# Transposing the spatial gating's weights at the end of the first feed-forward sub-layer

## The chip, the cores and the metric

The kernel runs on one core of a Trainium2 chip. The metric is the device time of one execution in microseconds (us). TensorE multiplies and transposes, ScalarE and VectorE work on tiles, GpSimd does a few small things, and SP's queue issues all loads and stores. Each engine takes its own instructions strictly in order and waits for the others by semaphores.

## The reference

One decoder layer over 256 tokens of width 2048: a feed-forward sub-layer, a mixer, a second feed-forward sub-layer, each with a norm before and behind it. The change concerns one weight of the mixer, `w_spatial`, and the place between the first sub-layer and the mixer.

```python
def spatial_gating(u, v, ln_g, ln_b, w_sp, b_sp):
    v = layer_norm(v, ln_g, ln_b).reshape(b_, nc, L, N_GMLP_GROUPS, GMLP_GROUP)
    w_causal = w_sp * jnp.tril(jnp.ones((L, L), dtype=w_sp.dtype))
    z = jnp.einsum('gts,bnsgc->bntgc', w_causal, v) + b_sp.T[None, None, :, :, None]
    return u * z.reshape(b_, s_, D_GMLP)
...
        x = sublayer(x, 0, ffn(0), 0.5)
        x = sublayer(x, 1, mixer, 1.0)
        x = sublayer(x, 2, ffn(1), 0.5)
```

There are 8 groups of weights of 128 x 128. TensorE contracts over the partitions, so the kernel needs each group transposed, and masked so that a token sees only earlier ones.

## The kernel before

All large weights stream once from memory. A load of 512 KB or less lands in one of 8 raw buffers (`rawp`); ScalarE casts it to a high part `wh` (line 315), VectorE computes the remainder `wl` (line 320), and TensorE takes three products for each tile of 128 rows (lines 338 to 340, `mm3`). Two token tiles of 128 tokens (`t` = 0, 1) share each weight tile. Large tiles of the activations live in 9 slots (`Slot`, shown as `big`) that are handed out in the order in which they were freed. [...]

A scheduling layer turns the code into one list for each engine and sets the semaphores. It may change the order a little between neighbours, so the place of an instruction is read from the built order and not from the code alone.

`boundary` is the edge between two sub-layers. It runs the last products for token tile 0 (`last_mm(0)`), norms and updates the residual `xt` (`post_norm_t`, lines 452 and 464), and in the meantime loads the first weights of the next projection. Then come the last products for token tile 1 (`last_mm(1)`). Behind them the first half of the next input for tile 0 is transposed (`to_h`, line 423), scaled by VectorE (line 404) and ScalarE (line 402) and split into `hh` (cast, line 373) and `hl` (line 374). With this half the first products of the next projection begin, while tile 1 is being updated; its sum of squares (line 385) goes to GpSimd for the power that gives `rstd` (line 391), and the normed tile (line 415) goes the same way.

Behind the edge, and in the middle of the mixer's first products, stand the mixer's small preparations, among them the spatial weights: a load into a slot (line 776), eight transposes into two banks (line 780), two copies to `wst` (line 781) and the causal mask on GpSimd:

```python
    nc.gpsimd.affine_select(out=wst, in_=wst, pattern=[[0, 8], [1, P]], compare_op=ALU.is_ge,
                            fill=0.0, base=0, channel_multiplier=-1)
```

`wst` is first used in `spatial`, well behind this.

Of the kernel before, what the change touches and what calls it, by code (L numbers as in the profile page):

```python
# [8 lines left out]
F32 = mybir.dt.float32  # L9
# [5 lines left out]
P = 128  # L15
# [17 lines left out]
def tile_layer(  # L33
# [6 lines left out]
    nc = tc.nc  # L40
# [3 lines left out]
    w_in, w_out, conv_w, conv_b = w_in[0], w_out[0], conv_w[0], conv_b[0]  # L44
    b_igate, b_fgate, g_mhnorm = b_igate[0], b_fgate[0], g_mhnorm[0]
    gmlp_ln_g, gmlp_ln_b = gmlp_ln_g[0], gmlp_ln_b[0]
    w_spatial, b_spatial = w_spatial[0], b_spatial[0]
# [7 lines left out]
    rawp = ctx.enter_context(tc.tile_pool(name="rawp", bufs=8))  # L55
# [9 lines left out]
    def nm(s):  # L65
        uid[0] += 1
        return f"{s}_{uid[0]}"

    def ps():
        return psp.tile([P, 512], F32, tag="ps", name=nm("ps"))  # L70
# [29 lines left out]
    ident = cpool.tile([P, P], F32, name="ident")  # L100
# [194 lines left out]
    def flush():  # L295
        while pending:
            pump()
# [120 lines left out]
    def to_h(sub, t, q, n):  # L418

        for i in range(0, 4, 2):  # L420
            pn = ps()
            for j in range(2):
                nc.tensor.transpose(pn[:, j * P:(j + 1) * P], n[:, (i + j) * P:(i + j + 1) * P], ident)
            ins = modulate(sub, q * 4 + i, 2, pn, t * P, (t + 1) * P, i == 2)
        return ins
# [51 lines left out]
            tiles += [(2 * half + j, wh[:, j, :], wl[:, j, :]) for j in range(2)]  # L477
        return tiles

    def boundary(last_mm, evac, times_g, xin, y, yp, free, early, ahead, nxt, src=None, c0=None, w=512):  # L480

        kept = [] if nxt is None else early + list(w_tiles(src, [(4, 2 * ahead, 4)], c0, w=w))
        last_mm(0)
        evac(0)
        r = rstd_of(yp[0])
        r0 = post_norm_t(y, 0, r, times_g, nxt is None, xin)
        if nxt is None:
            last_mm(1)  # L490
            evac(1)
            r = rstd_of(yp[1])
            post_norm_t(y, 1, r, times_g, True, xin)
            return None
        if ahead == 1:
            floor[0] = last_update[0]
            kept += list(w_tiles(src, [(6, 2, 6)], c0, w=w))
        n0 = [normed(0, q, r0) for q in range(2)]
        last_mm(1)
        for s_ in free:  # L500
            s_.free()
        banks = [ps(), ps()]
        evac(1)
        r = rstd_of(yp[1])
        to_h(nxt, 0, 0, n0[0])
        to_h(nxt, 0, 1, n0[1])
        for k, wh, wl in kept:
            tok_mm(k, wh, wl, 0, banks[0][:, 0:w])
        r1 = post_norm_t(y, 1, r, times_g, False, xin)
        pq = [[ps(), ps()] for _ in range(2)]  # L510
        for q in range(2):
            n = normed(0, 2 + q, r0, last_update[0])
            for k in range(4):
                transposed_to(pq[q], k, 0, n)
        n1 = [normed(1, q, r1) for q in range(2)]
        to_h(nxt, 1, 0, n1[0])
        floor[:] = to_h(nxt, 1, 1, n1[1])
        for k, wh, wl in kept[:4]:
            tok_mm(k, wh, wl, 1, banks[1][:, 0:w])
        n = normed(1, 2, r1)  # L520
        for k in range(4):
            transposed_to(pq[0], k, 1, n)
        modulate_q(nxt, 2, pq[0], False)
        for k, wh, wl in kept[4:]:
            tok_mm(k, wh, wl, 1, banks[1][:, 0:w])
        n = normed(1, 3, r1)
        for k in range(4):
            transposed_to(pq[1], k, 1, n)
        modulate_q(nxt, 3, pq[1], False)
        for s_ in y + xin + gg:  # L530
            s_.free()
        gg[0] = None
        return banks, 2
# [43 lines left out]
        pending.append(rest())  # L577
        return g

    def ffn(idx, supers, begun, xin, nxt, nxt_src=None, nxt_c0=None, nxt_w=512):  # L580

        y = None
        yp = [parts() for _ in range(NT)]

        def evac_y(si, q, t, bank):
            ys = y[t].t[:, q * 512:(q + 1) * 512]
            if si == 0:
                nc.scalar.copy(ys, bank)
            else:
                nc.vector.tensor_tensor(out=ys, in0=ys, in1=bank, op=ALU.add)  # L590
            if si == len(supers) - 1:
                sumsq(yp[t], q, ys)

        for si, blocks in enumerate(supers):
            gs = []
            n = len(blocks)
            for b, segs, part, banks in blocks:
                if si == 0 and begun is not None and not gs:
                    gb = proj_tok(w_ff_gate[idx], b * FB, begun)
                    ub = proj_tok(w_ff_up[idx], b * FB)  # L600
                elif part is not None:
                    gb = proj_tok(w_ff_gate[idx], b * FB, segs=segs, first=segs[0][0])
                    ub = proj_tok(w_ff_up[idx], b * FB, segs=segs, first=segs[0][0])
                    flush()
                    gs.append(swiglu_sum(gb, ub, part))
                    continue
                else:
                    gb = proj_tok(w_ff_gate[idx], b * FB, segs=segs, banks=banks and banks[0])
                    ub = proj_tok(w_ff_up[idx], b * FB, segs=segs, banks=banks and banks[1])
                flush()  # L610
                gs.append(Slot((P, 2, 4, S), F32R))
                pending.append(swiglu_evac(gs[-1], gb, ub))
            if y is None:
                y = [Slot((P, D)) for _ in range(NT)] if xin[0].__class__ is Half else [Half(t) for t in range(NT)]
            rows = [(4 * i, 4, 4 * b[0]) for i, b in enumerate(blocks)]

            def mms(k, wh, wl, t):
                g = gs[k // 4].t
                mm3(banks[t], g[:, 0, k % 4, t * P:(t + 1) * P], g[:, 1, k % 4, t * P:(t + 1) * P],
                    wh, wl, k == 0, k == 4 * n - 1)  # L620

            for q in range(4):
                banks = [ps(), ps()]
                if si == len(supers) - 1 and q == 2:
                    for s_ in xin:
                        s_.t
                if si == len(supers) - 1 and q == 3:
                    flush()
                    if side[0] is not None:
                        side[0].drain()  # L630
                    early = early_w(nxt_src, nxt_c0, nxt_w)
                    kept, slots = hold(w_ff_down[idx], rows, q * 512, NW if nxt is None else 3)

                    def last_mm(t):
                        for k, wh, wl in kept:
                            mms(k, wh, wl, t)

                    return boundary(last_mm, lambda t: evac_y(si, q, t, banks[t]), lambda t: times_gg(y, t, q), xin, y, yp, slots + gs,
                                    early, 1, nxt, nxt_src, nxt_c0, nxt_w)
                else:  # L640
                    for k, wh, wl in w_tiles(w_ff_down[idx], rows, q * 512):
                        for t in range(NT):
                            mms(k, wh, wl, t)
                    for t in range(NT):
                        later(evac_y, si, q, t, banks[t])
                        if si == len(supers) - 1:
                            later(times_gg, y, t, q)
            if si < len(supers) - 1:
                for g in gs:
                    g.free()  # L650
# [67 lines left out]
    supers = [[], [], []]  # L718
# [34 lines left out]
    xin = [Reload(t) for t in range(NT)]  # L753

    blocks = [(4718, 410), (4308, 410), (3896, 412), (3484, 412), (G0, 412)]
    begun = ffn(0, supers, None, xin, 1, w_in, *blocks[0])
    side[0] = None


# [10 lines left out]
    lng = Slot((P, 2, DM))  # L770
    nc.sync.dma_start(lng.t[:, 0, :], gmlp_ln_g.partition_broadcast(P))
    nc.sync.dma_start(lng.t[:, 1, :], gmlp_ln_b.partition_broadcast(P))
    wst_s = Slot((P, 8, P))
    wst = wst_s.t
    wspr = Slot((P, 8, P))
    nc.sync.dma_start(wspr.t, w_spatial.rearrange("g t s -> t g s"))
    for i in range(2):
        pw = ps()
        for j in range(4):
            nc.tensor.transpose(pw[:, j * P:(j + 1) * P], wspr.t[:, i * 4 + j, :], ident)  # L780
        nc.scalar.copy(wst[:, i * 4:i * 4 + 4, :], pw.rearrange("p (g t) -> p g t", t=P))
    nc.gpsimd.affine_select(out=wst, in_=wst, pattern=[[0, 8], [1, P]], compare_op=ALU.is_ge,
                            fill=0.0, base=0, channel_multiplier=-1)
    wspr.free()
    gbias = cpool.tile([P, 8], F32, name="gbias")
    nc.sync.dma_start(gbias[:, 0:4], b_igate.partition_broadcast(P))
    nc.sync.dma_start(gbias[:, 4:8], b_fgate.partition_broadcast(P))
# [275 lines left out]
    yp = [parts() for _ in range(NT)]  # L1063
    y = None
# [20 lines left out]
    y = [Slot((P, D)) for _ in range(NT)]  # L1085
    for q in range(4):
# [8 lines left out]
        else:  # L1095
            flush()
            side[0].drain()
            early = early_w(w_ff_gate[1], 0, 512)
# [44 lines left out]
```

## Time and profile before

| | |
|---|---|
| median of 3 runs | 1872.24 us (1871.8 to 1872.76) |
| the profiled execution | 1872.83 us, of which the span of the instructions is 1870.8 |
| TensorE busy | 1823.0 us, 97% of the span |
| VectorE, ScalarE, GpSimd busy | 1365.0, 853.6, 22.5 us |
| loaded and stored | 499.82 MB, 267 GB/s in the mean |
| granted clock of TensorE | 0.999 of full speed in the mean |

Busy time is summed for each engine over the whole span. It does not say where an engine waited, or for whom; that is read stretch by stretch. Times in the rows below count from the start of the span.

### The profile page before, as it was taken

To read this page: it belongs to the slowest core of one execution; us is meant where nothing else is said; L and a number is where in the kernel's file an instruction comes from. 1 tells how busy PE (TensorE), PEld (TensorE's weight loads), DVE (VectorE), ACT (ScalarE), POOL (GpSimd) and SP (SyncE) were. 2 spreads that over 40 slices of the span, in tenths; PEclk is the share of its full clock that TensorE was granted. 3 is DMA by queue.
4 is the path that set the end of the run, shared out by engine and by line. 5 is a ranking of instruction groups with operands and counts; after the bars stand their busy time and mean duration, and the time that the engine had idled before them with its cause. 6 is when DMAs were issued, how large, how long until landed. Compare 5 with 4: busy or idle time off the path is not lost.

```text
span 1870.8 us, 23057 instructions
## 1 busy us (share of the span) xinstructions
PE 1823.0 (97%) x8501; PEld 1523.7 (81%) x8501; DVE 1365.0 (73%) x1479; ACT 853.6 (46%) x1058; POOL 22.5 (1%) x42
## 2 busy tenths in 40 slices
PE   3999999999999999999999999999999999999998
PEld 2888888888888888799988887888888888888886
DVE  6888798788987888868898987555556555556455
ACT  3555444444443444655545446444444444334443
POOL 1000000000000000000000000000000000000000
PEclk9999999999999999999999999999999999999999
DMA  9999889999899999578689994776677776677662
GB/s 346 346 359 342 314 293 318 319 307 322 294 331 323 340 306 334 188 240 278 218 288 306 358 342 141 221 223 213 228 228 221 221 223 214 219 228 220 190 190 91
DMA packets 232617, 499.82 MB, mean 267 GB/s; under 512 B 16828, under 2 KB 28332, under 8 KB 231992
## 3 DMA queue, kind: packets, MB, share of 16 engines
q1 hardware_dynamic: 232504, 498.36, 79.9%
q8 instruction: 66, 1.08, 0.2%
q14 instruction: 47, 0.39, 0.1%
HBM read 496.19 MB, written 2.10 MB: 266 GB/s over the span
## 4 chain that ended last, share of the span: by engine, by line
PE 86%; issue 8%; DVE 3%; DMA 2%; POOL 1%; ACT 0%; DVEq 0%; POOLq 0%; ACTq 0%; SPq 0%
PE ps L338 28%; PE ps L339 28%; PE ps L340 28%; DVE acc L172 2%; PE ps L542 1%; DVE wl L320 1%; DMA raw<-in_w_ada_dram 1%; DMA raw<-in_w_ff_up_dram 0%; POOL rstd L391 0%; DMA raw<-in_w_ff_gate_dram 0%; DMA xt<-in_x_dram 0%; PE ps L197 0%; PE ps L930 0%; ACT wh L315 0%; POOL brs L808 0%
## 5 line engine op out<-in xcount | busy, mean ns | idle before, releaser
L320 DVE TENSOR_TENSOR wl<-raw,wh 128x1024 fp32r<-128x1024 f32 (+2 forms) x635 | 766.1, 1210 | 450.3 <-ACT wh L315 449.3
L315 ACT CAST wh<-raw 128x1024 fp32r<-128x1024 f32 (+2 forms) x637 | 662.6, 1043 | 864.1 <-PE ps L340 737.0
L338 PE MATMUL ps<-wh,hh 128*128 128x512 f32 (+2 forms) x1680 | 650.3, 390 | 1.5 <-ACT hh L373 1.5
L339 PE MATMUL ps<-wl,hh 128*128 128x512 f32 (+2 forms) x1680 | 649.3, 387 | 1.2 <-DVE wl L320 1.2
L340 PE MATMUL ps<-wh,hl 128*128 128x512 f32 (+2 forms) x1680 | 649.1, 386 | 0.0
L339 PEld LDWEIGHTS ps<-wl,hh 128*128 128x128 f32 x1680 | 316.5, 188 | 61.9 <-DVE wl L320 2.7
L340 PEld LDWEIGHTS ps<-wh,hl 128*128 128x128 f32 x1680 | 316.1, 188 | 60.5
L338 PEld LDWEIGHTS ps<-wh,hh 128*128 128x128 f32 x1680 | 315.9, 188 | 60.1 <-ACT hh L373 1.7
L172 DVE SCALAR_TENSOR_TENSOR acc<-raw,cs,acc 128x1024 f32<-128x1024 f32 x270 | 345.1, 1278 | 0.8 <-DVE parts L389 0.4
L338 PE MATMUL ps<-wh,big 128*128 128x512 f32 x804 | 314.6, 392 | 0.0
L339 PE MATMUL ps<-wl,big 128*128 128x512 f32 x804 | 313.1, 389 | 0.2 <-DVE wl L320 0.2
L340 PE MATMUL ps<-wh,big 128*128 128x512 f32 x804 | 313.1, 389 | 0.0
L339 PEld LDWEIGHTS ps<-wl,big 128*128 128x128 f32 x804 | 151.0, 188 | 31.8 <-DVE wl L320 1.0
L340 PEld LDWEIGHTS ps<-wh,big 128*128 128x128 f32 x804 | 150.9, 188 | 31.7
L338 PEld LDWEIGHTS ps<-wh,big 128*128 128x128 f32 x804 | 150.9, 188 | 30.6
L338 PE MATMUL ps<-hh,wh 128*128 128x256 f32 x128 | 37.6, 293 | 0.0
L680 ACT COPY big<-ps 128x512 f32<-128x512 f32 x32 | 18.7, 589 | 40.8 <-PE ps L340 39.5
L374 DVE TENSOR_TENSOR big<-ps,big 128x512 fp32r<-128x512 f32 x52 | 35.5, 683 | 1.3 <-ACT big L373 1.2
L340 PE MATMUL ps<-hh,wl 128*128 128x256 f32 x128 | 36.2, 283 | 0.0
L339 PE MATMUL ps<-hl,wh 128*128 128x256 f32 x128 | 36.2, 283 | 0.0
L373 ACT CAST big<-ps 128x512 fp32r<-128x512 f32 x52 | 30.1, 578 | 0.0
L385 ACT ACTIVATE t<-xt 128x512 f32<-128x512 f32 x32 | 20.0, 626 | 17.7 <-DVE xt L590 9.6
(194 smaller groups left out, 751.4 us busy)
## 6 DMA issues: line engine op xcount, KB each, us to landing
raw<-in_w_ada_dram SPq DMA_DIRECT2D x224, 512.0 KB, 5.3
raw<-in_w_ff_gate_dram SPq DMA_DIRECT2D x176, 512.0 KB, 4.5
raw<-in_w_ff_up_dram SPq DMA_DIRECT2D x176, 512.0 KB, 4.5
raw<-in_w_ff_down_dram SPq DMA_DIRECT2D x176, 512.0 KB, 5.1
raw<-in_w_ada_dram SPq DMA_DIRECT2D x128, 256.0 KB, 5.5
raw<-in_w_in_dram SPq DMA_DIRECT2D x48, 512.0 KB, 5.1
raw<-in_w_out_dram SPq DMA_DIRECT2D x32, 512.0 KB
raw<-in_w_in_dram SPq DMA_DIRECT2D x24, 412.0 KB, 4.8
```

The lines of the kernel that those rows point to most:

```text
L172: ins = nc.vector.scalar_tensor_tensor(a, raw[:, j, :, :], cs[:, k:k + 1], a, op0=ALU.mult, op1=ALU.add)
L315: behind(nc.scalar.copy(wh, rawv), floor[1])
L320: last_split[0] = nc.vector.tensor_tensor(out=wl, in0=rawv, in1=wh.bitcast(F32), op=ALU.subtract)
L338: nc.tensor.matmul(o, lh, rh, start=start, stop=False, skip_group_check=True)
L339: nc.tensor.matmul(o, lh, rl, start=False, stop=False, skip_group_check=True)
L340: nc.tensor.matmul(o, ll, rh, start=False, stop=stop, skip_group_check=True)
L373: act = nc.scalar.copy(dh, src)
L374: return nc.vector.tensor_tensor(out=dl, in0=src, in1=dh.bitcast(F32), op=ALU.subtract), act
L385: nc.scalar.activation(junk, src, AF.Square, scale=float(D) ** -0.5, accum_out=p[:, q + q // 3:q + q // 3 + 1])
L542: nc.tensor.transpose(pg[:, j * S + t * P:j * S + (t + 1) * P], gts[t][:, m * P:(m + 1) * P], ident)
L680: nc.scalar.copy(part.t.rearrange("p k s -> p (k s)")[:, u * 1024 + i * 512:u * 1024 + (i + 1) * 512], banks[i])
```

## The change

The load of the spatial weights and the eight transposes are issued from within `boundary`, between `last_mm(1)` and the first `to_h`; the load goes to a raw buffer and no longer to a slot. The two copies to `wst` are issued behind the first two `to_h`. The mask stays where it was in the code. The lines that went are those of the old place.

```diff
--- before.py
+++ after.py
@@ -477,7 +477,7 @@
             tiles += [(2 * half + j, wh[:, j, :], wl[:, j, :]) for j in range(2)]
         return tiles
 
-    def boundary(last_mm, evac, times_g, xin, y, yp, free, early, ahead, nxt, src=None, c0=None, w=512):
+    def boundary(last_mm, evac, times_g, xin, y, yp, free, early, ahead, nxt, src=None, c0=None, w=512, between=None):
 
 
 
@@ -499,11 +499,14 @@
         last_mm(1)
         for s_ in free:
             s_.free()
+        rest = between() if between is not None else None
         banks = [ps(), ps()]
         evac(1)
         r = rstd_of(yp[1])
         to_h(nxt, 0, 0, n0[0])
         to_h(nxt, 0, 1, n0[1])
+        if rest is not None:
+            rest()
         for k, wh, wl in kept:
             tok_mm(k, wh, wl, 0, banks[0][:, 0:w])
         r1 = post_norm_t(y, 1, r, times_g, False, xin)
@@ -577,7 +580,7 @@
         pending.append(rest())
         return g
 
-    def ffn(idx, supers, begun, xin, nxt, nxt_src=None, nxt_c0=None, nxt_w=512):
+    def ffn(idx, supers, begun, xin, nxt, nxt_src=None, nxt_c0=None, nxt_w=512, between=None):
 
         y = None
         yp = [parts() for _ in range(NT)]
@@ -636,7 +639,7 @@
                             mms(k, wh, wl, t)
 
                     return boundary(last_mm, lambda t: evac_y(si, q, t, banks[t]), lambda t: times_gg(y, t, q), xin, y, yp, slots + gs,
-                                    early, 1, nxt, nxt_src, nxt_c0, nxt_w)
+                                    early, 1, nxt, nxt_src, nxt_c0, nxt_w, between)
                 else:
                     for k, wh, wl in w_tiles(w_ff_down[idx], rows, q * 512):
                         for t in range(NT):
@@ -753,7 +756,26 @@
     xin = [Reload(t) for t in range(NT)]
 
     blocks = [(4718, 410), (4308, 410), (3896, 412), (3484, 412), (G0, 412)]
-    begun = ffn(0, supers, None, xin, 1, w_in, *blocks[0])
+    wst_s = [None]
+
+    def spatial_weights():
+
+        wspr = rawp.tile([P, 8, P], F32, tag="raw", name=nm("wspr"))
+        nc.sync.dma_start(wspr, w_spatial.rearrange("g t s -> t g s"))
+        pws = [ps(), ps()]
+        for j in range(8):
+            nc.tensor.transpose(pws[j // 4][:, (j % 4) * P:(j % 4 + 1) * P], wspr[:, j, :], ident)
+
+        def rest():
+            wst_s[0] = Slot((P, 8, P))
+            for i in range(2):
+                nc.scalar.copy(wst_s[0].t[:, i * 4:i * 4 + 4, :], pws[i].rearrange("p (g t) -> p g t", t=P))
+
+        return rest
+
+    begun = ffn(0, supers, None, xin, 1, w_in, *blocks[0], between=spatial_weights)
+    wst_s = wst_s[0]
+    wst = wst_s.t
     side[0] = None
 
 
@@ -770,18 +792,8 @@
     lng = Slot((P, 2, DM))
     nc.sync.dma_start(lng.t[:, 0, :], gmlp_ln_g.partition_broadcast(P))
     nc.sync.dma_start(lng.t[:, 1, :], gmlp_ln_b.partition_broadcast(P))
-    wst_s = Slot((P, 8, P))
-    wst = wst_s.t
-    wspr = Slot((P, 8, P))
-    nc.sync.dma_start(wspr.t, w_spatial.rearrange("g t s -> t g s"))
-    for i in range(2):
-        pw = ps()
-        for j in range(4):
-            nc.tensor.transpose(pw[:, j * P:(j + 1) * P], wspr.t[:, i * 4 + j, :], ident)
-        nc.scalar.copy(wst[:, i * 4:i * 4 + 4, :], pw.rearrange("p (g t) -> p g t", t=P))
     nc.gpsimd.affine_select(out=wst, in_=wst, pattern=[[0, 8], [1, P]], compare_op=ALU.is_ge,
                             fill=0.0, base=0, channel_multiplier=-1)
-    wspr.free()
     gbias = cpool.tile([P, 8], F32, name="gbias")
     nc.sync.dma_start(gbias[:, 0:4], b_igate.partition_broadcast(P))
     nc.sync.dma_start(gbias[:, 4:8], b_fgate.partition_broadcast(P))
```

In the built order three places differ. Names are the program's: `ps` is a bank, `big` a slot, `t2` a scratch tile, `xt` the residual, and the numbers tell tiles apart.

ScalarE, behind the last update of token tile 0, before:

```order
L385 ACTIVATE t2_1312_6369,parts_351_1726<-xt_96 128x512
L402 ACTIVATE t2_1317_6386<-ps_1316_6383,bm_118,am_117 128x128
L373 CAST hh_115<-t2_1315_6378 128x2x128
L402 ACTIVATE t2_1317_6386<-ps_1316_6383,bm_118,am_117 128x128
L402 ACTIVATE t2_1321_6402<-ps_1320_6399,bm_118,am_117 128x128
L373 CAST hh_115<-t2_1317_6386 128x2x128
L373 CAST hh_115<-t2_1319_6394 128x2x128
L402 ACTIVATE t2_1321_6402<-ps_1320_6399,bm_118,am_117 128x128
L373 CAST hh_115<-t2_1321_6402 128x2x128
```

ScalarE at the same place, of the change:

```order
L772 COPY big_1325_6419<-ps_1311_6368 128x512
L385 ACTIVATE t2_1315_6381,parts_351_1726<-xt_96 128x512
L402 ACTIVATE t2_1320_6398<-ps_1319_6395,bm_118,am_117 128x128 x2
L373 CAST hh_115<-t2_1318_6390 128x2x128
L373 CAST hh_115<-t2_1320_6398 128x2x128
L373 CAST hh_115<-t2_1322_6406 128x2x128
L402 ACTIVATE t2_1324_6414<-ps_1323_6411,bm_118,am_117 128x128 x2
L772 COPY big_1325_6419<-ps_1312_6369 128x512
L373 CAST hh_115<-t2_1324_6414 128x2x128
```

One copy of the spatial weights now stands ahead of the sum of squares of token tile 1 (the row with `parts_351`), the other ahead of the last of the four casts to `hh`; and both `L402` of the first pair stand ahead of the first cast.

GpSimd, from the `rstd` of token tile 0 on, before (`big_1496` is `umask`, `big_1354` is `wst`, `big_1583` is `vv`):

```order
L391 TENSOR_TENSOR rstd_1304_6318<-parts_1299_6302,nhalf_94 128x1
L380 MEMSET parts_1323_6433 128x1
L843 AFFINE_SELECT big_1496_7330<-onesr_90 128x128
L391 TENSOR_TENSOR rstd_1313_6373<-parts_351_1726,nhalf_94 128x1
L380 MEMSET parts_1767_8834 128x1
L391 TENSOR_TENSOR rstd_1328_6449<-parts_1323_6433,nhalf_94 128x1
L380 MEMSET parts_1768_8836 128x1
L970 MEMSET big_1583_7977 128x8
L782 AFFINE_SELECT big_1354_6569<-big_1354_6569 128x1024
```

GpSimd at the same place, of the change (`wst` is `big_1325`):

```order
L855 AFFINE_SELECT big_1496_7330<-onesr_90 128x128
L391 TENSOR_TENSOR rstd_1304_6318<-parts_1299_6302,nhalf_94 128x1
L380 MEMSET parts_1327_6448 128x1
L391 TENSOR_TENSOR rstd_1316_6385<-parts_351_1726,nhalf_94 128x1
L380 MEMSET parts_1767_8834 128x1
L795 AFFINE_SELECT big_1325_6419<-big_1325_6419 128x1024
L982 MEMSET big_1583_7977 128x8
L391 TENSOR_TENSOR rstd_1332_6464<-parts_1327_6448,nhalf_94 128x1
L380 MEMSET parts_1768_8836 128x1
```

The mask of `umask` went ahead of the first of the three `rstd`, and the mask of `wst` and the fill of `vv` went ahead of the last of them.

SP's queue, at the old place of the load, before:

```order
L157 DMA raw_6722<-in_w_ada_dram 128x1024
L771 DMA big_6566<-in_gmlp_ln_g_dram 128x1024
L772 DMA big_6566<-in_gmlp_ln_b_dram 128x1024
L776 DMA big_6570<-in_w_spatial_dram 128x8x128
L304 DMA raw_6724<-in_w_in_dram 128x2x410
```

SP's queue at the new place, of the change:

```order
L304 DMA raw_6251<-in_w_in_dram 128x2x410
L304 DMA raw_6320<-in_w_in_dram 128x2x410
L764 DMA wspr_6366<-in_w_spatial_dram 128x8x128
L304 DMA raw_6591<-in_w_in_dram 128x2x410
L304 DMA raw_6609<-in_w_in_dram 128x2x410
```

The load of the spatial weights moved ahead of seven loads of `w_in`. On TensorE nothing else moved than the eight transposes, and on VectorE one `L464` went behind two `L374`.

## Rows read from the trace of the kernel before

**Rows 1.** The chain that ended last, shares of the span by engine (page, part 4).
```profile
PE 86%; issue 8%; DVE 3%; DMA 2%; POOL 1%; ACT 0%; DVEq 0%; POOLq 0%; ACTq 0%; SPq 0%
```

**Rows 2.** Stretches, TensorE to GpSimd: us, busy us (instructions); then granted clock, DMA share, GB/s.
```profile
780.00:782.40 2.40, 1.04 (x10) 0.80 (x8) 1.99 (x6) 1.42 (x5) 0.71 (x2) 1.00 1.06 300
782.40:787.14 4.74, 4.74 (x24) 4.33 (x24) 4.74 (x11) 4.04 (x12) 0.23 (x2) 1.00 0.78 256
787.14:791.20 4.06, 2.58 (x18) 1.69 (x17) 3.21 (x11) 1.90 (x7) 0.65 (x2) 1.00 0.00 0
791.20:801.80 10.60, 10.60 (x58) 9.91 (x58) 9.98 (x18) 9.84 (x19) 0.00 (x0) 1.00 0.36 89
```

**Rows 3.** Timeline of TensorE: start us, busy us, line, operation, tiles, [wait and releaser].
```profile
779.77 0.39 PE L340 MATMUL ps<-big,big 128*128 128x512 f32 x1
780.00 1.03 PE L423 MATMUL ps<-ident,t 128*128 128x128 f32 x8
782.40 0.45 PE L338 MATMUL ps<-hh 128*128 128x410 f32 x1 [1.36 <-ACT hh L373]
...
791.20 0.45 PE L338 MATMUL ps<-hh 128*128 128x410 f32 x1 [0.21 <-ACT hh L373]
...
802.09 1.09 PE L780 MATMUL ps<-ident,big 128*128 128x128 f32 x8
802.94 0.43 PE L340 MATMUL ps<-wh,hl 128*128 128x410 f32 x1
```

**Rows 4.** Timeline of ScalarE over the edge and at the copies.
```profile
780.98 0.63 ACT L385 ACTIVATE t<-xt 128x512 f32<-128x512 f32 x1 [3.15 <-DVE xt L590]
...
781.61 0.44 ACT L402 ACTIVATE t<-ps,bm,am 128x128 f32<-128x128 f32 x1
781.95 0.39 ACT L373 CAST hh<-t 128x256 fp32r<-128x256 f32 x1
...
802.78 1.07 ACT L781 COPY big<-ps 128x512 f32<-128x512 f32 x2 [0.27 <-PE ps L780]
```

**Rows 5.** Timeline of VectorE over the edge.
```profile
780.81 0.72 DVE L404 TENSOR_SCALAR t<-ps,am,bm 128x128 f32<-128x128 f32 x2
...
782.46 0.41 DVE L374 TENSOR_TENSOR hl<-t,hh 128x256 fp32r<-128x256 f32 x1
...
784.06 0.74 DVE L452 SCALAR_TENSOR_TENSOR xt<-xt,rstd,big 128x512 f32<-128x512 f32 x1
...
788.75 0.88 DVE L415 TENSOR_SCALAR t<-xt,rstd 128x512 f32<-128x512 f32 x2 [0.67 <-POOL rstd L391]
```

**Rows 6.** Timeline of GpSimd over the edge and at the mask.
```profile
778.41 0.55 POOL L391 TENSOR_TENSOR rstd<-parts,nhalf 128x1 f32<-128x1 f32 x1 [3.95 <-DVE parts L389]
...
780.25 0.29 POOL L843 TENSOR_SCALAR_AFFINE_SELECT big<-onesr 128x128 f32<-128x128 f32 x1 [1.12 <-PE ps L340]
...
788.16 0.55 POOL L391 TENSOR_TENSOR rstd<-parts,nhalf 128x1 f32<-128x1 f32 x1 [5.47 <-DVE parts L389]
...
803.93 1.27 POOL L782 TENSOR_SCALAR_AFFINE_SELECT big<-big 128x1024 f32<-128x1024 f32 x1 [0.57 <-ACT big L781]
```

**Rows 7.** Timelines of GpSimd and VectorE where two masks run.
```profile
895.75 1.18 POOL L891 TENSOR_SCALAR_AFFINE_SELECT t<-t 128x512 f32<-128x512 f32 x1 [43.31 <-DMA raw<-in_w_in_dram]
895.74 0.68 DVE L898 TENSOR_TENSOR t<-t,t 128x512 f32<-128x512 f32 x1
...
907.81 0.64 POOL L891 TENSOR_SCALAR_AFFINE_SELECT t<-t 128x512 f32<-128x512 f32 x1 [10.88 <-DMA raw<-in_w_in_dram]
907.94 1.05 DVE L898 TENSOR_TENSOR t<-t,t 128x512 f32<-128x512 f32 x1
```

**Rows 8.** SP's queue, and the DMA's busy tenths in 40 parts of 779 to 800.
```profile
760.68 9.83 SPq L304 DMA_DIRECT2D raw<-in_w_in_dram  x7
...
780.20 0.38 SPq L776 DMA_DIRECT2D big<-in_w_spatial_dram  x1
...
DMA  9699999899999500000000000000000095938694
```

## The prediction

> **What bounds the kernel now.** I read the chain that ended last first: 86% of it is TensorE and 2% a transfer [rows 1], so time is won or lost where TensorE stands still, or by what it is given to do. Then I cut the edge between the first feed-forward sub-layer and the mixer into stretches [rows 2], because everything the change touches lies there. The reader should see three things. From 780.00 to 782.40 TensorE works 1.04 us of 2.40. From 787.14 to 791.20 it works 2.58 of 4.06. From 791.20 to 801.80 it works 10.60 of 10.60, and VectorE (9.98) and ScalarE (9.84) are nearly full too. So there are two waits, and behind them a stretch paced by TensorE. The eight transposes of the spatial weights stand behind that, at 802.09 [rows 3].
>
> What ends each wait I took from the engines' timelines. The first ends at 782.40 with ScalarE's first cast to `hh` (781.95, 0.39 us) [rows 3, 4]. The second ends at 791.20, behind one long chain: VectorE runs without a hole to 787.14, 4.74 us of 4.74 (the casts' remainders `hl` from 782.46 on, the `L452` updates of the second token tile from 784.06), then the last sum of squares, GpSimd's `rstd` at 788.16, VectorE's `L415` at 788.75, transposes, modulation and cast [rows 2, 3, 5, 6].
>
> **The change, part by part.**
>
> *Removed at 802.* Eight transposes start at 802.09 and the next product at 802.94 [rows 3]. The stretch is TensorE's, so their going is worth 0.85 us. The bounds: nothing, if ScalarE or VectorE, both nearly full just before [rows 2], set the pace once TensorE has less to do; 1.09, their whole busy time. I take 0.85, since each loses work there too or keeps it: the two copies on ScalarE go (1.07 us) [rows 4].
>
> *Added at 780.* The last product starts at 779.77 and the first `to_h` transpose at 780.00 [rows 3]. The eight new ones go between, so `to_h` begins 0.85 later, at 780.85. Of this, most lies in the first wait, which is ScalarE's and VectorE's:
> - ScalarE. The first copy can start when four transposes are done, which took 0.69 before (802.09 to 802.78) [rows 3, 4]: at 780.69. A copy holds ScalarE 0.48 (two take 1.07, one 0.59). The sum of squares behind it moves from 780.98 to 781.18. After it the order now has both `L402` ahead of the first cast, not one, and one takes 0.34 (781.61 to 781.95) [rows 4]. The first cast goes from 781.95 to 781.18 + 0.63 + 2 x 0.34 = 782.49 and ends at 782.88. The first product follows 0.06 behind, at 782.94 for 782.40.
> - VectorE. Its first modulation needs two transposes. With 0.85 / 8 = 0.107 us for one, that is 0.69 - 2 x 0.107 = 0.48 after 780.85: 781.33, against 780.81 [rows 5]. The first remainder `hl` waits for the cast: 782.94 for 782.46, so 0.48 late. From there the same instructions follow without a hole, whatever their order, so the second wait ends 0.48 later.
>
> Bounds for this part: nothing, if the copies found holes; 0.85 + 0.48 = 1.33, if the transposes and a copy came in full. I take 0.48.
>
> *Moved on GpSimd.* This queue's order changes twice. The mask of `umask` (0.29 us, at 780.25) [rows 6] now stands ahead of the `rstd` that the transposes at 780.00 need. It waits for a product twelve places before the last; at 0.23 us each (779.77 to 780.00) [rows 3] that is about 777.5 with the product's own 0.39 us, so it ends near 777.8, and that `rstd` starts at 778.41 [rows 6]. Nothing is paid. The mask of the spatial weights `wst` (1.27 us, at 803.93) [rows 6] now stands ahead of the `rstd` that ends the second wait, with the small fill of `vv`, which waits only for an earlier `L464`. What is queued behind it is that `rstd`, and VectorE's `L415`, TensorE's transposes and all of the mixer wait for it. The mask starts when the second copy is done. That copy stands behind three casts and two more `L402`: 782.49 + 3 x 0.39 + 2 x 0.34 = 784.34 at the latest, done 0.59 later, so the mask begins by 785.0. The `rstd` is asked for at about 788.16 + 0.48. So in the queue alone there is room for 1.27 us.
>
> But a neighbour can be held up. A mask over 512 columns took 0.64 us at 907.81; VectorE's `L898`, begun 0.13 behind it, took 1.05 where the same instruction, begun first, took 0.68 at 895.74. There it was the mask that grew, to 1.18 [rows 7]. Each time the later one ended as if it had begun to read when the other ended: the two take turns at something. VectorE's `L452` reads two tiles as `L898` does and stands back to back with others of its kind from 784.06 on [rows 2, 5]. If the mask gets its turn between two of them, the chain grows by the time that it holds; if it gets none, it runs in the hole that VectorE leaves before `rstd`, and `rstd` comes that much later. Both land on the second wait. The price: 0.64 - 0.13 = 0.51 for 512 columns [rows 7], twice that, less a fixed part, for 1024: I take 0.95. Bounds: nothing (it fits into holes), and 1.27 (its row before).
>
> [...]
>
> *Moved on SP's queue.* The spatial weights' transfer, issued at 780.20, now stands where the first of seven `w_in` loads was, at 760.68, and takes one of eight raw buffers. Before, all transfers had landed 14 of 40 parts into the stretch 779 to 800, by 786.4, so this one took at most 6.2 us [rows 8]. From 760.68 that is 767, with 13 us to spare before 780.00. The loads behind it land a buffer later; the last now waits for a raw buffer to be split, as the `w_ada` load did, and is not among the tiles of this stretch. One `w_ada` load moves behind the new transposes; its sum is not needed in this stretch. Nothing is paid; without that cover each us of lateness would be a us of TensorE's.
>
> *Sum.* -0.85 + 0.48 + 0.95 = +0.58 us. The profiled execution took 1872.83 (span 1870.8 and 2.0 around it) and would take 1873.4. It stands 0.6 above the median of the three runs, 1872.24, so I predict 1872.8. Behind 803 every engine's order is the same as before, and TensorE paces the rest [rows 1], so the shift goes through to the end.
>
> **The rivals.**
> 1. The mask costs nothing, because it finds holes on VectorE. Then -0.85 + 0.48 = -0.37: 1871.9. For it: the holes that the 0.48 opens. Against it: there is none before 787.14 now [rows 2].
> 2. The transposes and copies too are hidden in the first wait (1.36 us stand empty there) and the change does what its place suggests: -0.85, 1871.4. Against it: the wait is ScalarE's, and the copies go onto ScalarE.
> 3. All comes in full: -0.85 + 1.33 + 1.27 = +1.75: 1874.0. For it: both engines are in one chain here.
> [...]
>
> **How the numbers follow.** A measurement of this kernel tells a change from none at about 0.2%, 3.7 us. I give the forecast 0.52, rival 1 0.25, rival 2 0.08, rival 3 0.10, rival 4 0.03, and 0.02 to a gain over 3.7 us, which would need more than half of both stretches (2.40 and 4.06 us) to go. So faster 0.02, same 0.95, slower 0.03. The forecast's own range is 1872.2 to 1873.5. The range over the cases takes in rivals 1 and 3, and with the spread of the three runs (0.96 us) reaches from 1871.2 to 1874.2.
>
> **What the profile after would show.** Right: eight transposes at about 780.0 without a wait before them, the first product near 782.9, the mask on GpSimd by 785.0 with either itself or one of VectorE's `L452`/`L374` beside it some 0.9 us longer than in the rows here, the first product behind the second wait near 792.6 for 791.20, and no transposes but one at 801.9. Wrong: a wait of TensorE ahead of the new transposes (the transfer), a clock below 1.00, a mask that grows by nothing beside unchanged `L452`, or new idle time on TensorE near 803, which would mean that the 0.85 was not TensorE's to give back.

## The result and the profile after

The changed kernel took 1887.92 us in the median of 6 runs (1887.25 to 1889.4), the kernel before 1872.26 beside it (1871.77 to 1872.86): a ratio of 1.0083 [1.0072, 1.0094], 15.7 us slower. Forecast was 1872.8, with a range that ended at 1874.2. The profiled execution of after took 1889.05, of which the span is 1887.0, 16.2 more than before's.

At the edge itself things went as forecast. The timeline of TensorE of after; columns as in [rows 3]:

```profile
783.76 0.39 PE L339 MATMUL ps<-big,big 128*128 128x512 f32 x1
...
786.03 0.39 PE L340 MATMUL ps<-big,big 128*128 128x512 f32 x1
786.26 1.03 PE L767 MATMUL ps<-ident,wspr 128*128 128x128 f32 x8
787.13 1.04 PE L423 MATMUL ps<-ident,t 128*128 128x128 f32 x8
789.14 0.45 PE L338 MATMUL ps<-hh 128*128 128x410 f32 x1 [0.98 <-ACT hh L373]
...
798.77 0.45 PE L338 MATMUL ps<-hh 128*128 128x410 f32 x1 [0.21 <-ACT hh L373]
...
809.21 0.35 PE L339 MATMUL ps<-wl,hh 128*128 128x410 f32 x1
809.49 0.26 PE L790 MATMUL ps<-ident,t 48*128 48x48 f32 x1
809.67 0.46 PE L340 MATMUL ps<-wh,hl 128*128 128x410 f32 x1
```

The new transposes follow the last product with no wait. But that product starts at 786.03, and in [rows 3] the same one starts at 779.77: **6.26 us were lost before the first instruction that the diff moves on TensorE**. From there the edge adds 809.67 - 802.94 - 6.26 = 0.47, where 0.58 was forecast. The rest is lost behind it, a little at a time: the shift is -0.1 at the start, 2.0 at 358, 6.3 at 780, 8.5 at 1101 and 15.7 at 1840 of before's time.

What is slower shows in the page's costliest groups (last columns: busy us, mean ns of one, idle before). Before:

```profile
L338 PE MATMUL ps<-wh,hh 128*128 128x512 f32 (+2 forms) x1680 | 650.3, 390 | 1.5 <-ACT hh L373 1.5
L338 PE MATMUL ps<-wh,big 128*128 128x512 f32 x804 | 314.6, 392 | 0.0
L339 PE MATMUL ps<-wl,big 128*128 128x512 f32 x804 | 313.1, 389 | 0.2 <-DVE wl L320 0.2
L340 PE MATMUL ps<-wh,big 128*128 128x512 f32 x804 | 313.1, 389 | 0.0
```

And after:

```profile
L338 PE MATMUL ps<-wh,hh 128*128 128x512 f32 (+2 forms) x1680 | 650.1, 390 | 1.5 <-ACT hh L373 1.5
L338 PE MATMUL ps<-wh,big 128*128 128x512 f32 x804 | 319.4, 398 | 0.0
L339 PE MATMUL ps<-wl,big 128*128 128x512 f32 x804 | 318.1, 396 | 0.0
L340 PE MATMUL ps<-wh,big 128*128 128x512 f32 x804 | 317.9, 395 | 0.0
```

Products whose weights (the stationary operand) lie in `hh` are the same. The 2412 whose weights lie in a slot grew by 4.8 + 5.0 + 4.8 = 14.6 us, with no idle time before them. Measured from one start to the next, as they are paced, they went from 227 to 233 ns in the mean, 2412 x 6.2 ns = 15.0 us. Nothing in the diff names these products; they are those of `w_ff_down` and of the output projection, all over the program.

**What differs for them is an address.** One large tile, `vv`, is 8224 bytes long in each partition, the other slot tiles are at most 8192, and slot number 4 has a pool of its own for it:

```python
    VSLOT = 4
...
            self.i = free_slots.pop(0)
            pool = bigv if self.i == VSLOT else big
```

The changed kernel takes one slot fewer (the raw spatial weights), so by its turn `vv` gets slot 0, which lies first in `big` and grows from 8192 to 8224 bytes. By the addresses of the two built programs, the slots behind it then start 32 bytes higher (the first of them at 90272, not 90240), and so do the raw buffers, the scratch tiles and the pool of slot 4; `hh`, `hl` (from 16512 on), `wh` and `wl` (from 49280) stay. Slot 0 itself keeps its place, but in the changed kernel no product has its weights there.

### The profile page after: what moved, and what is told of

It is laid out like the page before. It is cut to its first block, busy times and chain, and to the rows that moved or that the text cites. A ratio compares the mean times of both kernels' runs of the same rounds, so it can differ in the third digit from the quotient of the medians.

```text
span 1887.0 us, 23058 instructions
## 1 busy us (share of the span) xinstructions
PE 1839.3 (97%) x8501; PEld 1525.3 (81%) x8501; DVE 1365.7 (72%) x1479; ACT 852.1 (45%) x1058; POOL 22.8 (1%) x42
## 4 chain that ended last, share of the span: by engine, by line
PE 88%; issue 8%; DVE 2%; DMA 1%; ACT 1%; POOL 1%; DVEq 0%; POOLq 0%; ACTq 0%
PE ps L338 28%; PE ps L340 28%; PE ps L339 28%; DVE acc L172 1%; PE ps L545 1%; DMA raw<-in_w_ada_dram 1%; DVE wl L320 0%; DMA xt<-in_x_dram 0%; ACT t L402 0%; POOL rstd L391 0%; DMA raw<-in_w_in_dram 0%; PE ps L440 0%; PE ps L197 0%; PE ps L942 0%; POOL brs L820 0%
## 5 line engine op out<-in xcount | busy, mean ns | idle before, releaser
L338 PE MATMUL ps<-wh,hh 128*128 128x512 f32 (+2 forms) x1680 | 650.1, 390 | 1.5 <-ACT hh L373 1.5
L339 PE MATMUL ps<-wl,hh 128*128 128x512 f32 (+2 forms) x1680 | 649.3, 386 | 1.2 <-DVE wl L320 1.2
L340 PE MATMUL ps<-wh,hl 128*128 128x512 f32 (+2 forms) x1680 | 649.5, 387 | 0.0
L339 PEld LDWEIGHTS ps<-wl,hh 128*128 128x128 f32 x1680 | 316.5, 188 | 62.3 <-DVE wl L320 2.7
L340 PEld LDWEIGHTS ps<-wh,hl 128*128 128x128 f32 x1680 | 315.9, 188 | 60.5
L338 PEld LDWEIGHTS ps<-wh,hh 128*128 128x128 f32 x1680 | 316.0, 188 | 59.8 <-ACT hh L373 1.7
L338 PE MATMUL ps<-wh,big 128*128 128x512 f32 x804 | 319.4, 398 | 0.0
L339 PE MATMUL ps<-wl,big 128*128 128x512 f32 x804 | 318.1, 396 | 0.0
L340 PE MATMUL ps<-wh,big 128*128 128x512 f32 x804 | 317.9, 395 | 0.0
L340 PEld LDWEIGHTS ps<-wh,big 128*128 128x128 f32 x804 | 151.0, 188 | 36.4
L339 PEld LDWEIGHTS ps<-wl,big 128*128 128x128 f32 x804 | 151.1, 188 | 36.3 <-DVE wl L320 0.8
L338 PEld LDWEIGHTS ps<-wh,big 128*128 128x128 f32 x804 | 151.0, 188 | 35.4
L338 PE MATMUL ps<-hh,wh 128*128 128x256 f32 x128 | 37.6, 293 | 0.0
L374 DVE TENSOR_TENSOR big<-ps,big 128x512 fp32r<-128x512 f32 x52 | 35.5, 684 | 1.3 <-ACT big L373 1.2
L340 PE MATMUL ps<-hh,wl 128*128 128x256 f32 x128 | 36.2, 283 | 0.0
L339 PE MATMUL ps<-hl,wh 128*128 128x256 f32 x128 | 36.2, 283 | 0.0
L391 POOL TENSOR_TENSOR rstd<-parts,nhalf 128x1 f32<-128x1 f32 x12 | 7.6, 631 | 1620.4 <-DVE parts L389 1620.4
```

The costliest lines, as they stand in the source:

```text
L338: nc.tensor.matmul(o, lh, rh, start=start, stop=False, skip_group_check=True)
L339: nc.tensor.matmul(o, lh, rl, start=False, stop=False, skip_group_check=True)
L340: nc.tensor.matmul(o, ll, rh, start=False, stop=stop, skip_group_check=True)
L374: return nc.vector.tensor_tensor(out=dl, in0=src, in1=dh.bitcast(F32), op=ALU.subtract), act
L391: nc.gpsimd.tensor_tensor(out=r, in0=p[:, 6:7], in1=nhalf[:, 0:1], op=ALU.pow)
```

## Experiments

Each time stands beside runs of the kernel before on the same chip. In the kernels with paddings line numbers are one to four higher (L338 is L339, L340 or L342). Where there are two paddings of 32 bytes, what lies behind the second is 64 bytes higher, so it keeps its place against a multiple of 64.

**1. The change with the old layout.** `vv` keeps a pool of its own, whichever slot it gets.

```diff
-    VSLOT = 4
+    VSLOT = 0
```

> The change as it is, but with the oversized slot (8224 bytes a partition, for `vv`) put where `vv` now lands, so that every slot and raw buffer stands at the address that it had before. Theory A (32 bytes of address): products with weights from a slot go back from 233 to 227 ns apart, the time to 1872.26 + 0.48 = 1872.7 (1872.2 to 1873.5), and the edge still costs what the prediction's walk gave. Theory B (the move itself, its transfer, its waits or a fall of the clock that it causes): 1888 as the change. Theory C (only the edge, without the mask on GpSimd in the way): 1871.9.

1873.72 us, ratio 1.0005 [0.9997, 1.0014]: no change that can be measured. The median is 0.2 above the range that was expected, and far from the 1888 of theory B. The 15 us are the layout's. This trace (span 1870.7) gives the forecast's terms without the drift; TensorE's timeline:

```profile
779.10 0.39 PE L340 MATMUL ps<-big,big 128*128 128x512 f32 x1
779.33 1.03 PE L767 MATMUL ps<-ident,wspr 128*128 128x128 f32 x8
780.20 1.04 PE L423 MATMUL ps<-ident,t 128*128 128x128 f32 x8
782.21 0.46 PE L338 MATMUL ps<-hh 128*128 128x410 f32 x1 [0.98 <-ACT hh L373]
...
791.84 0.45 PE L338 MATMUL ps<-hh 128*128 128x410 f32 x1 [0.20 <-ACT hh L373]
...
802.75 0.45 PE L340 MATMUL ps<-wh,hl 128*128 128x410 f32 x1
```

Against [rows 3], counted from the last product (779.10 for 779.77, so 0.67 is added to each): `to_h` 0.87 late, the first product 0.48, the end of the second wait 1.31, the first product behind the old place 0.48.

**2. The mask behind all three `rstd`** (with the old layout).

```diff
-    nc.vector.tensor_copy(v3, pt[:, 0:48])
+    v3_copy = nc.vector.tensor_copy(v3, pt[:, 0:48])
...
-    nc.gpsimd.affine_select(out=wst, in_=wst, pattern=[[0, 8], [1, P]], compare_op=ALU.is_ge,
-                            fill=0.0, base=0, channel_multiplier=-1)
+    behind(nc.gpsimd.affine_select(out=wst, in_=wst, pattern=[[0, 8], [1, P]], compare_op=ALU.is_ge,
+                                   fill=0.0, base=0, channel_multiplier=-1), v3_copy)
```

> As e1_vslot, and the mask of `wst` on GpSimd behind the three `rstd` of the edge. If the mask holds up VectorE in the edge as the prediction's third term says, 0.9 us less than e1_vslot: 1871.8. If that term is empty, the same as e1_vslot.

1872.2 us, ratio 1.0000 [0.9992, 1.0009]. In the trace the same four landmarks are 0.88, 0.49, 0.81 and 0.08 late. The mask now meets VectorE's `L415`; GpSimd and VectorE:

```profile
789.61 1.36 POOL L795 TENSOR_SCALAR_AFFINE_SELECT big<-big 128x1024 f32<-128x1024 f32 x1
789.53 1.72 DVE L415 TENSOR_SCALAR t<-xt,rstd 128x512 f32<-128x512 f32 x2 [0.67 <-POOL rstd L391]
```

Two `L415` take 1.72 for the 0.88 of [rows 5], but TensorE's second wait ends only 0.81 - 0.49 = 0.32 later, for 0.83 in experiment 1. So the mask's place is worth 0.5 us at the second wait (1.31 - 0.81) and 0.4 at the last landmark (0.48 - 0.08), and it is not free at this one.

**3. Transposes behind `to_h`, copies behind the first products** (and the mask late, the old layout).

```diff
-        rest = between() if between is not None else None
...
         to_h(nxt, 0, 1, n0[1])
-        if rest is not None:
-            rest()
+        rest = between() if between is not None else None
         for k, wh, wl in kept:
             tok_mm(k, wh, wl, 0, banks[0][:, 0:w])
+        if rest is not None:
+            rest()
```

> As e8_mask_late, and the eight transposes behind the two `to_h`, in TensorE's empty 1.36 us, with the copies behind the first casts. If the second term (0.48) is what transposes and copies ahead of `to_h` cost, the whole 0.85 of the removal is left: 1871.4. If the 0.85 is not TensorE's to give back, 1872.3.

1872.16 us, ratio 0.9998 [0.9989, 1.0007]. TensorE's timeline:

```profile
779.39 1.04 PE L423 MATMUL ps<-ident,t 128*128 128x128 f32 x8
780.26 1.04 PE L767 MATMUL ps<-ident,wspr 128*128 128x128 f32 x8
781.78 0.45 PE L338 MATMUL ps<-hh 128*128 128x410 f32 x1 [0.49 <-ACT hh L373]
```

The landmarks are 0.0, 0.0, 0.5 late and at last 0.24 early: the eight transposes fit into the first wait. The second wait is still late, and two `L415` take 1.71 beside the mask here too, so the whole 0.85 that was expected of this form does not come. This is the best form of the change that the runs give, and its gain is far below what a measurement of this kernel can tell.

**4. The kernel before with the change's layout.** Paddings of 32 bytes ahead of `big` and ahead of the constants; slots, raw buffers and scratch tiles all lie 32 higher.

```diff
+    pad0 = ctx.enter_context(tc.tile_pool(name="pad0", bufs=1))
+    pad0.tile([P, 8], F32, name="gap0")
     big = ctx.enter_context(tc.tile_pool(name="big", bufs=1))
...
+    pad1 = ctx.enter_context(tc.tile_pool(name="pad1", bufs=1))
+    pad1.tile([P, 8], F32, name="gap1")
     cpool = ctx.enter_context(tc.tile_pool(name="cpool", bufs=1))
```

> The kernel before, nothing moved, with 32 unused bytes a partition ahead of the slots: slots, raw buffers, scratch tiles and sums stand 32 bytes higher, as in the change. Theory A: 2412 products with weights from slots at 6.2 ns more each, 15.0 us, so 1887.3 (1886.5 to 1888). Theory B: 1872.3, as before.

1888.34 us, ratio 1.0084 [1.007, 1.0098]: the whole loss, without a line of the change (0.3 above the range expected).

**5. The slots alone.** The second padding stands ahead of the raw buffers.

```diff
+    pad0.tile([P, 8], F32, name="gap0")
     big = ...
+    pad1.tile([P, 8], F32, name="gap1")
     rawp = ...
```

> The kernel before with the eight slots alone 32 bytes higher, all behind them back on multiples of 64. If it is the slots (weights of TensorE's products): +15 us, 1887. If it is the raw buffers or scratch tiles (casts, remainders, transfers): 1872.3.

1887.53 us, ratio 1.0079 [1.0064, 1.0094].

```profile
L342 PE MATMUL ps<-wh,big 128*128 128x512 f32 x804 | 319.5, 398 | 0.0
```

**6. All but the slots**: raw buffers, scratch and `w_ada` tiles 32 higher.

```diff
+    pad0.tile([P, 8], F32, name="gap0")
     rawp = ...
+    pad1.tile([P, 8], F32, name="gap1")
     bigv = ...
```

> The kernel before with raw buffers, scratch tiles and sums alone 32 bytes higher, the slots where they were. If it is the slots: 1872.3. If it is the raw buffers or scratch tiles: 1887.

1873.89 us, ratio 1.0006 [0.9996, 1.0015]. So it is the slots, and not the raw buffers or scratch tiles that ScalarE, VectorE and the transfers read and write.

```profile
L342 PE MATMUL ps<-wh,big 128*128 128x512 f32 x804 | 314.8, 392 | 0.0
```

**7. `hh` and `hl` alone** 32 off.

```diff
+    pad0.tile([P, 8], F32, name="gap0")
     hpool = ...
+    pad1.tile([P, 8], F32, name="gap1")
     wsp = ...
```

> The kernel before with `hh` and `hl` alone 32 bytes off a multiple of 64. They are the weights (the operand that is loaded) of about 5090 products of 410 to 512 columns. If any weights 32 bytes off cost 6.2 ns a product: +31 us, 1904. If it is something of the slots alone: 1872.3.

1899.84 us, ratio 1.0145 [1.0128, 1.0162]. `wh`, `wl` and the slots lie 64 higher here, so `hh` lies 32 lower against the streaming operand and the slots lie at no distance. Now it is the other products, one line of three each:

```profile
L342 PE MATMUL ps<-wh,hh 128*128 128x512 f32 (+2 forms) x1680 | 658.3, 394 | 1.5 <-ACT hh L377 1.5
L342 PE MATMUL ps<-wh,big 128*128 128x512 f32 x804 | 314.7, 392 | 0.0
```

The loss is 27.0 where some 31 were expected. The 456 products of 410 and 412 columns were counted in, and they did not slow down: the median from one start to the next is 187 ns for those of 410, before and here. One form of them, before and in this experiment:

```profile
L338 PE MATMUL ps<-wh,hh 128*128 128x412 f32 x96 | 33.5, 349 | 0.0
```

```profile
L342 PE MATMUL ps<-wh,hh 128*128 128x412 f32 x96 | 33.5, 349 | 0.0
```

**8. `wh` and `wl` alone**, the streaming operand of both kinds of product.

```diff
+    pad0.tile([P, 8], F32, name="gap0")
     wsp = ...
+    pad1.tile([P, 8], F32, name="gap1")
     big = ...
```

> The kernel before with `wh` and `wl` alone 32 bytes off. They are the operand that streams through in nearly all products of 512 columns, and the weights in 384 of 256 columns. If the weights' address matters and the streaming operand's doesn't: +0 to +2.4 us (384 x 6.2 ns), 1872.3 to 1874.7. If the streaming operand's address matters as much: some 7400 products x 6.2 ns, +46 us, 1918.

1915.0 us, ratio 1.0223 [1.0208, 1.0238]: both kinds are slow, and the loss, 42.2, is close to that of experiments 5 and 7 together (14.7 + 27.0 = 41.7). The slots lie 64 higher here, so they are 32 higher than the streaming operand, and `hh` is 32 lower.

```profile
L342 PE MATMUL ps<-wh,hh 128*128 128x512 f32 (+2 forms) x1680 | 658.4, 395 | 1.5 <-ACT hh L377 1.5
L342 PE MATMUL ps<-wh,big 128*128 128x512 f32 x804 | 319.4, 398 | 0.0
```

My first theory, that weights at such an address are slow, fell here: the weights lie where they were against a multiple of 64, and the products are slow. Two were left: any operand that lies off is slow, or the two operands must lie alike (theory C).

**9. All operands of the products 32 higher.**

```diff
+    pad0.tile([P, 8], F32, name="gap0")
     hpool = ...
+    pad1.tile([P, 8], F32, name="gap1")
     cpool = ...
```

> The kernel before with every tile of the products, streaming operand (wh, wl) and both kinds of weights (hh, hl and slots) alike, 32 bytes higher. Theory C (a product of 512 columns takes 233 ns for 227 when its streaming operand and its weights lie differently modulo 64 bytes): nothing differs any more, products 227 ns, 1872.3, within 1.5. Rival (any operand that is 32 off in itself makes the product slow): all products 233 ns, 1915 or more, as with wh and wl alone.

1873.03 us, ratio 0.9999 [0.999, 1.0008]. Every operand is off, and nothing is slow:

```profile
L342 PE MATMUL ps<-wh,hh 128*128 128x512 f32 (+2 forms) x1680 | 649.8, 389 | 1.5 <-ACT hh L377 1.5
L342 PE MATMUL ps<-wh,big 128*128 128x512 f32 x804 | 314.5, 392 | 0.0
```

**10. `wh`, `wl` and the slots 32 higher.**

```diff
+    pad0.tile([P, 8], F32, name="gap0")
     wsp = ...
+    pad1.tile([P, 8], F32, name="gap1")
     rawp = ...
```

> The kernel before with wh, wl and the slots 32 bytes higher, hh and hl where they were. Theory C (streaming operand and weights differ): only the products with hh and hl as weights differ and take 233 ns, those with slots 227; the time is that of hh and hl alone being moved, 1899.8, within 2. Rival (any operand off): both kinds at 233 ns, 1915 as with wh and wl alone.

1898.94 us, ratio 1.0138 [1.0121, 1.0154]. The same slots that are slow in experiment 5 are fast once `wh` and `wl` are moved along with them:

```profile
L342 PE MATMUL ps<-wh,hh 128*128 128x512 f32 (+2 forms) x1680 | 658.6, 395 | 1.5 <-ACT hh L377 1.5
L342 PE MATMUL ps<-wh,big 128*128 128x512 f32 x804 | 314.6, 392 | 0.0
```

It is the distance of the two operands that counts. The next four ask modulo what.

**11. The slots 64 higher** (paddings as in 5, of 16 elements in place of 8).

```diff
-    pad0.tile([P, 8], F32, name="gap0")
+    pad0.tile([P, 16], F32, name="gap0")
```

> The kernel before with the slots alone 64 bytes higher. If the place modulo 64 decides: products with slots 227 ns, 1872.3, within 1.5. If the place modulo 128 (or any difference) decides: 233 ns, 1887.5, as with 32 bytes.

1887.76 us, ratio 1.0078 [1.0063, 1.0093]: my guess of 64 in theory C fell.

**12. The slots 128 higher**, with all behind them.

```diff
+    pad0.tile([P, 32], F32, name="gap0")
     big = ...
```

> The kernel before with the slots (and everything behind them) 128 bytes higher, wh, wl, hh and hl where they were. If the difference between streaming operand and weights counts modulo 128 bytes: products with slots 227 ns, 1872.5, within 1.5. If it counts modulo more, or if any difference counts: 233 ns, 1887.5, as with 32 and 64 bytes.

1885.61 us, ratio 1.0067 [1.005, 1.0084]. Still slow, if a little less. All large products of the kernel before lie at a distance of 0 modulo 512, which led to theory D.

**13. The slots 256 higher.**

```diff
-    v2 = cpool.tile([P, 64], F32, name="v2")
+    v2 = pad0.tile([P, 64], F32, name="v2")
```

> The kernel before with the slots 256 bytes higher (the 256 bytes are one small tile, v2, that lay behind them). Theory D (products are fast where weights and streaming operand start at the same place modulo 512 bytes, as all large products of the kernel before do): 256 apart is slow, 232 to 233 ns, 1885 to 1888. Rival (modulo 256): 227 ns, 1872.5, within 1.5.

1872.23 us, ratio 0.9998 [0.9989, 1.0008]. Theory D's 512 fell; 256 will do. The lines of experiments 11, 12 and 13:

```profile
L342 PE MATMUL ps<-wh,big 128*128 128x512 f32 x804 | 319.2, 398 | 0.0
```

```profile
L340 PE MATMUL ps<-wh,big 128*128 128x512 f32 x804 | 318.9, 397 | 0.0
```

```profile
L339 PE MATMUL ps<-wh,big 128*128 128x512 f32 x804 | 314.6, 392 | 0.0
```

**14. The slots 512 higher.**

```diff
-    ident = cpool.tile([P, P], F32, name="ident")
+    ident = pad0.tile([P, P], F32, name="ident")
```

> The kernel before with the slots 512 bytes higher (the 512 bytes are the identity, which lay behind them). Theory D (modulo 512): 227 ns, 1872.5, within 1.5. Rival (the slots must not be moved at all, or the distance counts modulo more than 512): 232 to 233 ns, 1885 to 1888.

1873.23 us, ratio 1.0003 [0.9993, 1.0012]. The line of experiment 13 reads the same here.

All of it in one table; the distance is that of weights from streaming operand, modulo 256, and ns are the mean from one start to the next for products of 512 columns, intervals of 300 ns and more left out:

| kernel | distance: `hh`, slots | ns: `hh`, slots | us more than before |
|---|---|---|---|
| before, 1 to 3, 6, 9, 13, 14 | 0, 0 | 227, 227 | -0.6 to 1.1 |
| after, 4, 5 | 0, 32 | 227, 233 | 14.7 to 15.7 |
| 11 | 0, 64 | 227, 233 | 14.7 |
| 12 | 0, 128 | 227, 232.6 | 12.6 |
| 7, 10 | -32, 0 | 233, 227 | 27.0, 25.9 |
| 8 | -32, 32 | 233, 233 | 42.2 |

## Why the prediction was wrong

**The step that failed** is at its start and its end: that "everything the change touches lies there", at the edge, and that "Behind 803 every engine's order is the same as before, and TensorE paces the rest [rows 1], so the shift goes through to the end". The order is indeed the same, and TensorE does pace it. But an order says which instruction comes next, not where its operands lie, and I took their durations for given: the sum has no term for them, and no reason is given why it should be nothing. The runs showed 14.6 us in its place, 2412 products at about 6 ns more each. The change took a slot out of the rotation, `vv` moved into another, and that changed the size of a slot and the address of all behind it. Experiment 1 takes this away and the loss is gone; experiment 4 puts it alone into the kernel before, and the loss is there. None of the rivals was about memory.

**The terms at the edge held**, by the trace of experiment 1, with after's (less 6.26) the same within 0.02:
- Removed at 802: 0.85 forecast, 1.31 - 0.48 = 0.83 measured (0.73 and 0.74 in experiments 2 and 3).
- Added at 780: the transposes delay `to_h` by 0.87 (0.85 forecast), the first product by 0.48 (0.48 was taken; 782.94 - 782.40 = 0.54 on its own row). ScalarE's first copy began in after at 786.89, which is 780.63, forecast 780.69.
- The mask: 0.95 forecast, 1.31 - 0.48 = 0.83 measured. It was `L374` that was held; GpSimd and VectorE of after:

```profile
790.96 1.48 POOL L795 TENSOR_SCALAR_AFFINE_SELECT big<-big 128x1024 f32<-128x1024 f32 x1 [1.83 <-ACT big L772]
791.40 1.31 DVE L374 TENSOR_TENSOR hl<-t,hh 128x256 fp32r<-128x256 f32 x1
```

One `L374` takes 0.41 in [rows 5], here 1.31, so 0.90 more (0.42 in experiment 2, with the mask behind it); and the mask began at 790.96 - 6.26 = 784.70, "by 785.0". Rival 1 (nothing) and rival 3 (all 1.27) are both off. That 0.95 came so near was partly luck: in [rows 7] `L898` grew by 1.05 - 0.68 = 0.37, and not by the 0.51 that the prediction took from there, and where in the mask its victim would begin, on which the price hangs, was not worked out. What was left of the mask was 0.51 in [rows 7] and is 1.48 - 0.44 = 1.04 here; both times the other instruction grew by 0.14 less than that. `L374` began 0.44 into the mask's 1.48 and ended 0.27 behind it. The `L452` ahead of it, which ran beside the mask's first 0.5, from 790.74 on, took 0.75, for 0.74 in [rows 5]. So the price is below the mask's whole time.
- The sum: +0.58 forecast, +0.48 in experiment 1. Its median lies 1.0 above before's, with an interval of the ratio (0.9997 to 1.0014) that holds both 0 and the sum.
- The transfer was in time: no wait ahead of `L767`.
- Rival 4, the one with 0.03, stood for a fall of TensorE's clock at this edge. Neither before's nor after's trace shows one there. The stretches of after that answer to [rows 2]:

```profile
786.26:789.14 2.88, 1.91 (x17) 1.67 (x15) 2.14 (x7) 2.25 (x7) 0.65 (x2) 1.00 0.94 289
789.14:793.98 4.84, 4.83 (x24) 4.33 (x24) 4.84 (x9) 3.35 (x10) 1.53 (x2) 1.00 0.54 202
793.98:798.77 4.79, 2.45 (x17) 1.66 (x17) 3.94 (x13) 2.63 (x10) 0.65 (x2) 1.00 0.00 0
798.77:808.50 9.73, 9.73 (x54) 9.20 (x55) 9.10 (x17) 9.66 (x18) 0.00 (x0) 1.00 0.32 89
```

The granted clock is 1.00 in all four, as in [rows 2], and the two stretches with the transposes grew from 2.40 and 4.06 us to 2.88 and 4.79.

The span's 16.2 us come out as 14.6 (products with slots), 0.5 (the edge) and 1.0 (a dip of the clock at the next edge, below): 16.1, the parts being good to some tenths.

## What to carry to other kernels

Before a blind forecast of a change that allocates or frees differently, compare the addresses of the two built programs as well as their order: one tile that is 32 bytes longer than its neighbours moved all behind it, and cost some 30 times what the edit itself did (15.0 us for 0.48). Keep the weights and the streaming operand of products of 512 columns at the same place modulo 256 bytes (here 227 ns from start to start at distances of 0, 256 and 512, and 232.6 to 233 at 32, 64, 128 and -32), and give odd-sized tiles a pool at the end that they get by name, not by their turn. When a span grows, first line up the same instructions in both traces: a shift that grows steadily ahead of the edit is not the edit's.

## What was not expected of the hardware

**Products depend on where their two operands lie against each other.** With 512 columns and 128 x 128 weights of 4 bytes the mean distance between starts is 227 ns at 0 modulo 256 bytes (0, 256 and 512 were run), 233 at 32, 64 and -32, and 232.6 at 128; no other distance was run. In after's own trace the held products `big,big`, whose two operands both lie 32 higher, keep 227 ns (783.76 to 786.03 in the first rows above, ten of them), beside `wh,big` at 233; of that run of eighteen, the first five, right behind a product with `wh`, took 228 to 236. Narrower products did not slow down: those of 410 and 412 columns at a distance of -32 (experiment 7: 187 ns from start to start for 410, and 349 ns busy for one of 412, both as before), and the 384 of 256 columns with `wh`, `wl` as weights (median 120 ns before, 117 at a distance of 32 in experiment 10; the `L338` among them are busy 293 ns in the mean before, and 292 at that distance in experiments 7 and 8). Where in the chip the two meet isn't shown, nor whether the weights that matter are a product's own or the next one's, which alternate too seldom here to tell. The weight loads' own records don't grow (188 ns in both), only the time between them (last column); before, then after:

```profile
L339 PEld LDWEIGHTS ps<-wl,big 128*128 128x128 f32 x804 | 151.0, 188 | 31.8 <-DVE wl L320 1.0
```

```profile
L339 PEld LDWEIGHTS ps<-wl,big 128*128 128x128 f32 x804 | 151.1, 188 | 36.3 <-DVE wl L320 0.8
```

**The clock dipped at the next edge in after and in experiment 14**, behind 3.5 us in which TensorE does little but eight transposes (1132.00 to 1135.54 in after). Stretches of after and of experiment 14, whose kernel has nothing of the change:

```profile
1136.00:1140.00 4.00, 4.00 (x13) 3.11 (x13) 3.94 (x8) 2.81 (x9) 0.00 (x0) 0.63 0.00 0
```

```profile
1126.50:1130.00 3.50, 3.50 (x11) 2.74 (x10) 3.44 (x7) 2.31 (x8) 0.00 (x0) 0.57 0.00 0
```

And of before, where the same transposes stand between 1123.32 and 1126.94:

```profile
1124.00:1128.00 4.00, 2.12 (x13) 1.67 (x14) 3.37 (x10) 2.71 (x9) 1.14 (x4) 1.00 0.02 7
1128.00:1132.00 4.00, 4.00 (x19) 3.34 (x18) 3.94 (x8) 2.82 (x9) 0.00 (x0) 1.00 0.00 0
```

The granted clock is 0.63 and 0.57 in the mean of the first two stretches, and 1.00 before. In after the first eight products behind the transposes take 3.50 us from start to start for 1.93 before, six of them 427 ns for 227: 1.6 us more in all. After's shift grew by only 1.06 across that edge (8.54 at 1101, 9.60 at 1140 of before's time), about 0.1 of it from products with slots, so the dip cost the span about 1.0: TensorE waited less behind it (0.36 before, nothing in after, ahead of the next six `L423`). As experiment 14 has the dip too, it is no part of the change; what sets it off is not shown.
